# A split weight's low half, made by accumulating transfers instead of GpSimd subtractions

## The chip, the cores and the metric

The kernel runs on one core of one Trainium2 chip. The metric is the device time of one execution in microseconds. It was run three times before the change.

## The reference

One layer of a hybrid encoder, for 256 tokens of width 1024, everything in float32:

```python
u = rmsnorm(h, norm1_w)
rx, rg, qkv, z, a_in, b_in, ga, gb = split_columns(u @ w_in, IN_WIDTHS)
# branch A: convolution, RG-LRU scan, gelu gate, projection
y_a = (gelu(rg) * rglru(conv(rx) + b, ...)) @ w_branch_a
# branch B: convolution + SiLU on q, k, v, chunked gated delta rule, gated norm, projection
y_b = (rmsnorm(gated_delta_rule(q, k, v, g, beta)) * silu(z)) @ w_branch_b
h = h + (sigmoid(ga) * y_a + sigmoid(gb) * y_b) @ w_out
h = h + memory_cross_attention(rmsnorm(h), rmsnorm(mem), w_cq, w_ckv, w_co)
h = h + hierarchical_moe(rmsnorm(h), ...)   # 64 experts, two for each token
return rmsnorm(h, norm_f_w)
```

The products with `w_in`, `w_branch_a`, `w_branch_b`, `w_out`, `w_cq`, `w_ckv` and `w_co` are what the change touches; the experts' weights (3 matrices of 2 MB for each of 64 experts) are not.

## The kernel before

The work has two parts. The first is the dense part: all projections, the two branches, the attention and the router. The second streams the weights of all 64 experts through the chip, in order, and computes each expert on up to 32 gathered tokens.

In the dense part the weights come in 66 units. A unit is one call of `load_w` (L157 to L172): 1024 KB of one weight matrix, 128 partitions by 2048 columns, or 640 KB in the eight units of branch A's projection. SP's queue (L162) loads it into the buffer `raw`, of which there are two. TensorE multiplies numbers of the type fp32r; to keep float32's precision each weight is split into a high half, which is the weight rounded to fp32r, and a low half, which is what the rounding left. The unit is split in two pieces `j`, each in a buffer `whl` of 128 by 2 by 1024: index 0 is the high half, index 1 the low half. There are four such buffers, so a unit uses the two of the unit two before it. ScalarE makes both pieces' high halves (L169). The low half of the first piece is made by VectorE, that of the second by GpSimd (L170), each as `raw` minus the high half.

`dense` (L174 to L180) then does, for each of the k rows of a unit, three matmuls: high weight by high activation (L178), high weight by low activation (L179), low weight by high activation (L180). A unit is two output columns `m` of 8 rows each, so 48 matmuls, or 30 in branch A's projection (one column of 10 rows). Rows 0 to 3 read the first piece, rows 4 to 7 the second: TensorE first reads the second piece's low half in the fifteenth matmul of a unit. L412 to L414 (values of the attention) and L189 to L191 (`dense_two`) are the same three products in other orders.

Which instruction comes when on each engine is decided by a planner that reads the program in order. Where the program says `tc.high_priority()`, as around the split, instructions are put ahead of others that are ready. Semaphores between the engines are added by it. Each engine and each queue works through its list in order; SP's queue holds the raw loads (L162) and the experts' loads (L1068 to L1080). A raw load waits until everything that reads its buffer's old contents is done.

The results of a unit leave PSUM by ScalarE and VectorE. For the convolutions of branch B that is a scaled copy by ScalarE (L309), three multiply-adds by VectorE for each of two columns (L313), a tanh by ScalarE (L462) and two multiply-adds by VectorE (L465). PSUM has four buffers for units.

The dense part's memory is given up in two steps: the early pool before the attention (`estack.close()`), which makes room for four buffers `ra` of 2 MB of expert weights, and the rest (`wstack.close()`) after the last unit, which makes room for six more, `rb`. From then on ten buffers are a ring: after each expert three more loads are issued, into the buffers of loads that are done with.

Of the kernel before, what the change touches and what calls it, by code (L numbers as in the profile page):

```python
# [8 lines left out]
FT = mybir.dt.float32  # L9
FR = mybir.dt.float32r  # L10
I32 = mybir.dt.int32
AF = mybir.ActivationFunctionType
OP = mybir.AluOpType
# [28 lines left out]
def hybrid_kernel(ctx: ExitStack, tc: tile.TileContext, A, out, dbg=None, until=99):  # L42
    nc = tc.nc
    V, SC, G, T = nc.vector, nc.scalar, nc.gpsimd, nc.tensor
# [112 lines left out]
    def load_w(src, k=8, m=256, hi=(SC, SC), lo=(V, G), loads=1):  # L157

        raw = wp.tile([128, 2048], FT, name="raw", bufs=2)[:, :k * m]
        n = k * m // loads  # L160
        for j in range(loads):
            nc.sync.dma_start(raw[:, j * n:(j + 1) * n], src[:, j * n:(j + 1) * n])  # L162
        kh = k // 2
        pieces = []
        with tc.high_priority():
            for j in range(2):
                w = wp.tile([128, 2, 1024], FR, name="whl", bufs=4)[:, :, :kh * m]
                r = raw[:, j * kh * m:(j + 1) * kh * m]
                (hi[j].copy if hi[j] is SC else hi[j].tensor_copy)(w[:, 0], r)  # L169
                lo[j].tensor_sub(w[:, 1], r, w[:, 0].bitcast(FT))  # L170
                pieces.append(w.rearrange("p s (k m) -> p s k m", k=kh))
        return lambda s_, i, ms: pieces[i // kh][:, s_, i % kh, ms]  # L172

# [52 lines left out]
    mt_ = early("memx").rearrange("p (c t) -> p c t", c=8)  # L226
    nc.sync.dma_start(mt_[:, :4], A["memT"][:, :4])
    wkv = [load_w(A["wkv"][0], loads=2)]
    nc.sync.dma_start(mt_[:, 4:], A["memT"][:, 4:])
    um_ = early("umh", FR), early("uml", FR)  # L230
# [25 lines left out]
    for un_ in range(4):  # L256
        w = wkv[0] if un_ == 0 else load_w(A["wkv"][un_])
        p = bank()
        for m in range(2):
            dense(p[:, m * 256:m * 256 + 256], w, m, um)  # L260
        SC.copy(KT[:, 2 * un_:2 * un_ + 2], two(p))
# [57 lines left out]
    def five(name, dt=FT):  # L319
        return early(name, dt)[:, :HB * 256].rearrange("p (b t) -> p b t", b=HB)  # L320
# [25 lines left out]
    for un_ in range(5):  # L346
        w = load_w(A["win"][un_])
        p = bank()
        for m in range(2):
            dense(p[:, m * 256:m * 256 + 256], w, m, u1)  # L350
        for m in range(2):
            r = un_ * 2 + m
            conv(xc[r // HB][:, r % HB], p[:, m * 256:m * 256 + 256], P("rcw", 4 * r, 4), P("rcb", r))
    gg = [five("gg0"), five("gg1")]
    for un_ in range(5):
        w = load_w(A["win"][5 + un_])
# [8 lines left out]
        for m in range(2):  # L365
            r = un_ * 2 + m
# [3 lines left out]
    for h in range(2):  # L370
        tr, ti = five("tr"), five("ti")
        for b in range(HB):
            r = h * HB + b
# [7 lines left out]
        for b in range(HB):  # L381
            r = h * HB + b
# [14 lines left out]
        hi, lo = five("ghh", FR), five("ghl", FR)  # L397
# [6 lines left out]
    for un_ in range(4):  # L404
        w = load_w(A["wkv"][4 + un_])
# [45 lines left out]
    for un_ in range(12):  # L451
        if un_ in (1,):
            z_unit((1,).index(un_))
        w = load_w(A["win"][10 + un_])
# [15 lines left out]
    for m in range(8):  # L470
        w = load_w(A["wa"][m], k=RB, m=128)
# [80 lines left out]
    src = blkT.rearrange("p (s q r) -> p s q r", s=16, q=2)  # L552
# [102 lines left out]
    for c in range(4):  # L655
# [35 lines left out]
        if c < 3:  # L691
# [5 lines left out]
            for h in range(8):  # L697
                src = pS[h % 2][:, h // 2 * 128:h // 2 * 128 + 128]
# [43 lines left out]
    for c0, n in ((0, 2), (2, 2), (4, 2), (6, 1), (7, 1)):  # L742
        if c0 % 2 == 0:
            w = load_w(A["wb"][c0 // 2])
# [22 lines left out]
    for c0, n in ((0, 2), (2, 2), (4, 2), (6, 1), (7, 1)):  # L767
        if c0 % 2 == 0:
            w = load_w(A["wo"][c0 // 2])
# [65 lines left out]
    for un_ in range(4):  # L835
        w = load_w(A["wcq"][un_])
# [43 lines left out]
    for un_ in range(4):  # L880
        w = load_w(A["wco"][un_])
# [522 lines left out]
```

## Time and profile before

| | |
|---|---|
| Median of 3 runs | 1501.56 us (1496.18 to 1501.62) |
| Profiled execution | 1500.7 us, span 1498.9 us |
| TensorE (matmuls) busy | 1113.3 us, 74% of the span |
| VectorE busy | 548.0 us, 37% |
| ScalarE busy | 352.1 us, 23% |
| GpSimd busy | 197.5 us, 13% |
| DMA | 477.40 MB, mean 318 GB/s |
| Chain that ended last | DMA 55% of the span |
| Granted TensorE clock, mean | 0.886 of full speed |

The profile is of one execution. PE is TensorE, DVE is VectorE, ACT is ScalarE, POOL is GpSimd, SP is SyncE, whose queue issues loads. A row of a group names a line of the kernel, the engine, the operation, the tile written and the tiles read, shapes, and how often; a row of a timeline begins with the start and the duration in us. Idle time of an engine is put down to what it waited for.

### The profile page before, as it was taken

How to read it: one execution, taken by the hardware profiler on the slowest of the kernel's cores; microseconds unless marked ns; L12 is line 12 of the kernel's file. 1: busy time of each engine (PE TensorE's matmuls, PEld its weight loads, DVE VectorE, ACT ScalarE, POOL GpSimd, SP SyncE). 2: the span in 40 equal slices, each digit the busy share in tenths (PEclk: the TensorE clock that was granted, in tenths of full speed). 3: DMA queues.
4: the chain of work that ended last, by engine and by line, in shares of the span. 5: the costliest groups of instructions: out<-in, count | busy, mean ns of one | idle time of the engine just before them, and what ended most of it. 6: DMA issues, size and time to landing. Idle time of an engine off the chain costs nothing.

```text
span 1498.9 us, 33205 instructions
## 1 busy us (share of the span) xinstructions
PE 1113.3 (74%) x14941; PEld 932.0 (62%) x14941; DVE 548.0 (37%) x1217; ACT 352.1 (23%) x746; POOL 197.5 (13%) x107
## 2 busy tenths in 40 slices
PE   6899988889999987876666665766656757566575
PEld 5899878779798975654544543544544535354453
DVE  7877688685466532221111211111201111112022
ACT  5356745424444520100000000000000000000011
POOL 2333333441135310000000000000000000000000
PEclk9799999988999998997897888888979889798898
DMA  6343444431147857999999999999999999999995
GB/s 253 118 170 132 138 144 134 148 113 57 38 162 300 327 212 304 426 424 426 426 425 426 425 427 425 425 427 426 425 426 425 427 425 425 426 426 427 426 425 195
DMA packets 42001, 477.40 MB, mean 318 GB/s; under 512 B 4480, under 2 KB 7168, under 8 KB 9856
## 3 DMA queue, kind: packets, MB, share of 16 engines
q1 hardware_dynamic: 40560, 472.56, 77.0%
q8 instruction: 119, 1.95, 0.5%
q10 hardware_dynamic: 1296, 2.68, 0.5%
q14 instruction: 26, 0.21, 0.0%
HBM read 474.17 MB, written 1.05 MB: 317 GB/s over the span
## 4 chain that ended last, share of the span: by engine, by line
DMA 55%; PE 5%; issue 1%; SPq 1%; DVE 0%; ACT 0%; DVEq 0%; ACTq 0%
DMA rb<-weu 11%; DMA rb<-wed 11%; DMA rb<-weg 10%; DMA ra<-wed 10%; DMA ra<-weu 8%; DMA ra<-weg 5%; PE gd L1107 2%; PE gd L1127 1%; PE gd L1098 1%; SPq L1080 1%; PE mm L1175 0%; PE mm L1143 0%; ACT fsq L1296 0%; PE sm L1090 0%; PE gd L1280 0%
## 5 line engine op out<-in xcount | busy, mean ns | idle before, releaser
L1107 PE MATMUL gd<-rb,xy 128*32 128x128 f32 x4864 | 184.0, 317 | 112.8 <-DMA rb<-weu 55.0
L1107 PEld LDWEIGHTS gd<-rb,xy 128*32 128x32 f32 x4864 | 162.2, 128 | 140.1 <-DMA rb<-weu 63.6
L170 POOL TENSOR_TENSOR whl<-raw,whl 128x1024 fp32r<-128x1024 f32 (+1 forms) x66 | 159.8, 2422 | 343.2 <-ACT whl L169 338.3
L1116 DVE SCALAR_TENSOR_TENSOR hid<-hid,gd 128x128 f32<-128x128 f32 x64 | 18.4, 288 | 446.9 <-ACT hid L1115 446.9
L1107 PE MATMUL gd<-ra,xy 128*32 128x128 f32 x3168 | 122.1, 320 | 76.7 <-DMA ra<-weu 39.3
L178 PE MATMUL mm<-u1h,whl 128*128 128x256 f32 x544 | 163.2, 300 | 9.8 <-DVE cvt L313 9.8
L1107 PEld LDWEIGHTS gd<-ra,xy 128*32 128x32 f32 x3168 | 106.9, 129 | 94.5 <-DMA ra<-weu 44.9
L180 PE MATMUL mm<-u1h,whl 128*128 128x256 f32 x544 | 161.3, 297 | 2.6 <-DVE whl L170 2.5
L179 PE MATMUL mm<-u1l,whl 128*128 128x256 f32 x544 | 160.7, 295 | 0.0
L169 ACT CAST whl<-raw 128x1024 fp32r<-128x1024 f32 (+1 forms) x132 | 131.1, 1008 | 105.2 <-PE mm L180 87.7
L1115 ACT ACTIVATE hid<-gd 128x128 f32<-128x128 f32 x64 | 17.8, 278 | 525.0 <-PE gd L1107 525.0
L1132 DVE COPY xy<-gd 32x256 f32<-32x256 f32 x126 | 52.6, 418 | 228.5 <-PE gd L1127 201.9
L1127 PE MATMUL gd<-rb,hid 128*32 128x256 f32 x1216 | 89.8, 445 | 61.4 <-DMA rb<-wed 41.2
L1132 ACT COPY xy<-gd 32x256 f32<-32x256 f32 x126 | 45.9, 364 | 306.0 <-DVE xy L1132 306.0
L178 PEld LDWEIGHTS mm<-u1h,whl 128*128 128x128 f32 x544 | 110.0, 202 | 12.3 <-issue 6.3
L180 PEld LDWEIGHTS mm<-u1h,whl 128*128 128x128 f32 x544 | 109.8, 202 | 5.1 <-DVE whl L170 2.9
L179 PEld LDWEIGHTS mm<-u1l,whl 128*128 128x128 f32 x544 | 109.8, 202 | 0.8 <-issue 0.2
L170 DVE TENSOR_TENSOR whl<-raw,whl 128x1024 fp32r<-128x1024 f32 (+1 forms) x66 | 86.0, 1302 | 55.9 <-ACT whl L169 55.6
L976 POOL TENSOR_TENSOR gpw<-goh,ew 128x512 f32<-128x512 f32 x8 | 8.4, 1049 | 735.2 <-PE sm L1138 680.7
L1127 PEld LDWEIGHTS gd<-rb,hid 128*32 128x32 f32 x1216 | 45.8, 123 | 95.1 <-issue 62.3
L1127 PE MATMUL gd<-ra,hid 128*32 128x256 f32 x800 | 61.1, 456 | 36.5 <-DMA ra<-wed 23.7
L1098 PEld LDWEIGHTS gd<-goh,hm 128*128 128x128 f32 x512 | 61.0, 192 | 14.5 <-issue 14.5
(421 smaller groups left out, 1786.0 us busy)
## 6 DMA issues: line engine op xcount, KB each, us to landing
rb<-weu SPq DMA_DIRECT2D x38, 2048.0 KB, 39.2
rb<-wed SPq DMA_DIRECT2D x38, 2048.0 KB, 39.2
rb<-weg SPq DMA_DIRECT2D x38, 2048.0 KB, 39.1
ra<-weg SPq DMA_DIRECT2D x26, 2048.0 KB, 39.2
ra<-weu SPq DMA_DIRECT2D x25, 2048.0 KB, 39.2
ra<-wed SPq DMA_DIRECT2D x25, 2048.0 KB, 39.2
raw<-win SPq DMA_DIRECT2D x34, 1024.0 KB, 4.9
raw<-wkv SPq DMA_DIRECT2D x7, 1024.0 KB, 5.0
```

Of the source, the lines that this page charges most:

```text
L169: (hi[j].copy if hi[j] is SC else hi[j].tensor_copy)(w[:, 0], r)
L170: lo[j].tensor_sub(w[:, 1], r, w[:, 0].bitcast(FT))
L178: T.matmul(p, w(0, i, ms), u(0, i), start=(i == 0), stop=False)
L179: T.matmul(p, w(0, i, ms), u(1, i), start=False, stop=False)
L180: T.matmul(p, w(1, i, ms), u(0, i), start=False, stop=(i == k - 1))
L1080: nc.sync.dma_start(last_columns(t, q), src[:, q].rearrange("(p j) n -> p j n", p=128))
L1098: T.matmul(o, hm[:, tt, c * 128:c * 128 + 128], g[:, tt], start=(tt == 0), stop=(tt == 1))
L1107: m = T.matmul(p[32 * j:32 * j + 32, o:o + 128], x[:, c], w(c)[:, j * 128:j * 128 + 128], start=(c == 0), stop=(c == 7), tile_position=(0, ...
L1115: SC.activation(tg, p[:, :128], AF.Tanh, scale=0.5)
L1116: V.scalar_tensor_tensor(th, tg, 1.0, p[:, :128], op0=OP.add, op1=OP.mult)
L1127: T.matmul(p[32 * q:32 * q + 32, :256], ht[:, 32 * j:32 * j + 32], w(j)[:, o:o + 256], start=(j == 0), stop=(j == 3), tile_position=(0, 32 ...
L1132: (SC.copy if q % 2 else V.tensor_copy)(Y[r:r + 32, q * 256:q * 256 + 256], p[32 * q:32 * q + 32, :256])
```

## The change

For the pieces whose low half GpSimd made, ScalarE now writes the negated high half into the place of the low half, and a transfer on GpSimd's queue adds the same weights to it, straight from the weight matrix in device memory. The pieces whose low half VectorE makes stay as they are.

```diff
                 (hi[j].copy if hi[j] is SC else hi[j].tensor_copy)(w[:, 0], r)
-                lo[j].tensor_sub(w[:, 1], r, w[:, 0].bitcast(FT))
+                if lo[j] is G:
+
+                    SC.activation(w[:, 1], w[:, 0].bitcast(FT), AF.Copy, scale=-1.0)
+                    G.dma_start(w[:, 1], src[:, j * kh * m:(j + 1) * kh * m], accum_op=OP.add)
+                else:
+                    lo[j].tensor_sub(w[:, 1], r, w[:, 0].bitcast(FT))
                 pieces.append(w.rearrange("p s (k m) -> p s k m", k=kh))
```

## Rows read from the trace of the kernel before

**Rows 1.** The page: span, ScalarE's and GpSimd's load in 40 slices, the subtractions
```profile
span 1498.9 us, 33205 instructions
...
PE 1113.3 (74%) x14941; PEld 932.0 (62%) x14941; DVE 548.0 (37%) x1217; ACT 352.1 (23%) x746; POOL 197.5 (13%) x107
...
ACT  5356745424444520100000000000000000000011
POOL 2333333441135310000000000000000000000000
...
L170 POOL TENSOR_TENSOR whl<-raw,whl 128x1024 fp32r<-128x1024 f32 (+1 forms) x66 | 159.8, 2422 | 343.2 <-ACT whl L169 338.3
```

**Rows 2.** Chain that ended last, in time: start us, us, what
```profile
571.79 1.49 PE gd L1107 x21
...
645.42 38.85 DMA ra<-weg
```

**Rows 3.** Stretches, us: busy us (instructions) by engine, granted clock, DMA share, GB/s
```profile
450.00:500.00 50.00, 46.61 (x366) 45.62 (x365) 34.68 (x47) 23.84 (x35) 29.89 (x23) 0.97 0.83 320
...
550.00:575.00 25.00, 11.09 (x115) 8.14 (x117) 10.23 (x60) 1.78 (x8) 1.50 (x2) 0.63 0.63 255
...
650.00:1450.00 800.00, 518.84 (x9233) 386.21 (x9230) 137.05 (x405) 63.37 (x193) 6.29 (x6) 0.85 1.01 426
```

**Rows 4.** Timelines, one unit at full pace: start us, us, engine, line [idle before]
```profile
83.43 1.05 ACT L169 CAST whl<-raw 128x1024 fp32r<-128x1024 f32 x1 [0.40 <-PE mm L180]
...
84.55 2.40 POOL L170 TENSOR_TENSOR whl<-raw,whl 128x1024 fp32r<-128x1024 f32 x1 [3.35 <-ACT whl L169]
90.31 2.41 POOL L170 TENSOR_TENSOR whl<-raw,whl 128x1024 fp32r<-128x1024 f32 x1 [3.35 <-ACT whl L169]
...
90.61 0.28 PE L180 MATMUL mm<-u1h,whl 128*128 128x256 f32 x1
```

**Rows 5.** One line's instructions: ScalarE activation of 128x1024, ns min/median/max
```profile
L514 ACT ACTIVATE dt<-dt x1: 1053/1053/1053, 295.9 to 295.9; 128x1024 f32<-128x1024 f32 x1
```

**Rows 6.** DMA issues (KB, us to landing), 450 to 500 us last; SP's issue, ns
```profile
raw<-win SPq DMA_DIRECT2D x34, 1024.0 KB, 4.9
...
raw<-wa SPq DMA_DIRECT2D x8, 640.0 KB, 3.8
...
raw<-wo SPq DMA_DIRECT2D x2, 1024.0 KB, 5.7
...
L162 SPq DMA_DIRECT2D raw<-win x34: 327/328/328, 28.9 to 383.3; - x34
```

**Rows 7.** Waits of SP's queue to 600 us: us in total, times, longest
```profile
SPq L162 <- POOL whl L170: 164.3, 54, 10.6
```

**Rows 8.** Timelines, two units with little to spare
```profile
181.20 2.41 POOL L170 TENSOR_TENSOR whl<-raw,whl 128x1024 fp32r<-128x1024 f32 x1 [7.19 <-ACT whl L169]
...
183.66 0.39 PE L180 MATMUL mm<-u1h,whl 128*128 128x256 f32 x1
...
487.63 2.50 POOL L170 TENSOR_TENSOR whl<-raw,whl 128x1024 fp32r<-128x1024 f32 x1 [1.08 <-ACT whl L169]
...
491.18 0.28 PE L180 MATMUL mm<-u2h,whl 128*128 128x256 f32 x1
```

**Rows 9.** Timelines, one unit of branch A's projection
```profile
252.93 0.73 ACT L169 CAST whl<-raw 128x640 fp32r<-128x640 f32 x1 [0.65 <-PE mm L180]
...
258.00 0.28 PE L180 MATMUL mm<-ghh,whl 128*128 128x256 f32 x1
```

**Rows 10.** Timelines of VectorE and GpSimd in the convolutions of branch B
```profile
215.85 0.41 DVE L465 SCALAR_TENSOR_TENSOR kf<-cth,cvt 128x256 f32<-128x256 f32 x1
...
216.58 2.54 DVE L465 SCALAR_TENSOR_TENSOR kf<-cth,cvt 128x256 f32<-128x256 f32 x1
...
216.43 2.40 POOL L170 TENSOR_TENSOR whl<-raw,whl 128x1024 fp32r<-128x1024 f32 x1 [4.83 <-DMA raw<-win]
223.66 2.40 POOL L170 TENSOR_TENSOR whl<-raw,whl 128x1024 fp32r<-128x1024 f32 x1 [4.83 <-ACT whl L169]
```

**Rows 11.** Waits of TensorE to 600 us: us in total, times, longest
```profile
PE mm L178 <- DVE cvt L313: 9.8, 6, 3.7
```

## The prediction, made before the run

> **What bounds the kernel now.** I read the page's heads first, then the chain of waits in order of time, the stretches, the waits of TensorE, and last the timelines of single weight units. The heads show a span in two parts: ScalarE and GpSimd are busy almost only in the first 14 or 15 of 40 slices [rows 1]. The chain shows what ends the span: from 645 us on it is one expert weight transfer behind the other, joined without gaps [rows 2], and between 650 and 1450 us the DMA engines are fully busy at 426 GB/s [rows 3]. That part is bytes divided by rate, and the change leaves its bytes alone. What the change touches lies in the first 15 slices, the dense part with its 66 weight units of `load_w`. How long those take sets when the last staging memory is given up and the first expert can run: between 550 and 575 us the DMA engines are only 0.63 busy and TensorE works 11 of 25 us [rows 3], so nothing there takes up a late start. I therefore pass a delay of the dense part on to the end one to one.
>
> In the dense part TensorE is the bound, and each unit's chain runs beside it. One unit at full pace shows it [rows 4]: ScalarE starts the second half's high part at 83.43 (1.05 us), when TensorE has left the slot; GpSimd subtracts from 84.55 for 2.40 us, to 86.95; TensorE first reads that low half at 90.61. So 3.66 us are to spare, and the next subtraction starts at 90.31: 5.76 us a unit.
>
> **What the change does to this chain.** Per unit it takes away one subtraction on GpSimd (66 of them, 2.42 us on average, 159.8 us in all [rows 1]) and adds one ScalarE pass and one accumulating transfer of 512 KB (320 KB in branch A's eight units), 33 MB in all. None of these 2.42 us is on the path at full pace, so their removal alone is worth nothing there. GpSimd's list waits at the same place as before, one ScalarE pass later; behind it stand only GpSimd's other 38 us of work (197.5-159.8 [rows 1]). A wait for the transfer at L180 is worse placed: TensorE works in order, and all later matmuls stand behind it.
>
> The ScalarE pass costs 1.05 us: the one ACTIVATE of that shape in the trace [rows 5]. The transfer can be issued at 83.43+1.05+1.05+0.07 = 85.60, and must have landed at 90.61. It has 5.0 us, which I call the allowance; D is its time from the end of the ScalarE pass to the landing. If D is longer, TensorE waits. The delay goes around a loop of two units, since a slot is used by every second unit, so at full pace a unit costs (D-5.0)/2.
>
> D has no row of its own. The nearest rows are the raw loads on SP's queue: 4.9 us from issue to landing for 1024 KB, 3.8 for 640 KB [rows 6], so by the line through both 3.4 us for 512 KB. An addition needs the old contents as well; if reading them counts like bytes, the transfer weighs 1024 KB: 4.9. I take 4.2. GpSimd as the issuer has no row either: SP's issue takes 0.33 us [rows 6], already in these figures, and a GpSimd pass over such a tile 2.40 [rows 4]; the extra is between 0 and 2.4 us, and I take 1.0, nearer to SP's, since a request is no pass over data. Third, the raw buffer. SP's next raw load waits for the subtraction on GpSimd in 54 cases [rows 7]. With the change the buffer is free when ScalarE has made the high half, about 1 us ahead of the accumulating transfer, so the 1024 KB load and the addition are in flight together in every unit. The load's own bytes take 1024 KB / 426 GB/s = 2.5 us [rows 3]; sharing costs between 0 and 1.2 us (half of it), I take 0.6. D = 4.2+1.0+0.6 = 5.8 us, with ends at 3.4 and 4.9+2.4+1.2 = 8.5.
>
> The Trainium skill, "Collectives: The Full Stack", section "The bandwidth ceiling: the fold count and why AG ≠ RS ≠ AR", says that an add inside the transfer emits two reads for each write, both on the same ring, and so moves at half a copy's rate. No row here shows it. By it the transfer would weigh 1024 KB, my 4.2 would become 4.9, and the sum would be some 14 us more.
>
> **The sum at D = 5.8.**
> - Units at full pace: I count 25 outside branch A, from the one of rows 4 to the one whose subtraction starts at 487.63 [rows 8], whose low half was ready at most 3.7 us before TensorE read it. Each (5.8-5.0)/2 = 0.4: +10.
> - Branch A's eight units: ScalarE 252.93, 0.73 us a pass, need at 258.00 [rows 9]: allowance 258.00-252.93-2*0.73-0.07 = 3.5. The smaller transfer takes 0.6 less, 5.2. Each (5.2-3.5)/2 = 0.85: +7.
> - Two units where nothing was to spare [rows 8]: 181.20+1.05+5.8 = 188.1 against a need at 183.66, and 487.63+1.05+5.8 = 494.5 against 491.18: 4.4+3.3, less the 0.8 that they have above: +7.
> - A gain: while GpSimd subtracts from 216.43, VectorE's L465 takes 2.54 us where the same instruction took 0.41 a moment before; there the subtractions come every 7.23 us instead of 5.76 [rows 10], and TensorE waits 9.8 us in six waits for VectorE's convolution [rows 11]. With no GpSimd subtraction this stall goes. The next bound is the transfer, 5.76+0.4 = 6.16 a unit. Six units: 6*(7.23-6.16) = -6.4.
> - Between 450 and 500 us the first expert transfers run beside the dense part: DMA share 0.83 [rows 3], a raw load takes 5.7 us there instead of 4.9 [rows 6]. For eight units I add 1 us to D, halved as above: +4 (0 if the load is the later one to suffer, 8 if nothing is halved).
> - ScalarE does 66 more passes in order, 67 us beside the 352 us of [rows 1]. It idled for most of this (it waits on TensorE 0.4 us or more ahead of each high half [rows 4]), but conversions of the convolutions stand behind the new pass. I add 3 (0 to 13: 12 convolution units at 1.05).
>
> Together 10+7+7-6.4+4+3 = +24.6. The profiled execution took 1500.7 us (1498.9 of span), 0.9 under the median shown, so 1500.7+24.6 = 1525, forecast slower.
>
> At D = 3.4 only the tight units wait (2.0+0.9) and six units gain 6*(7.23-5.76) = 8.8: 1495. At D = 8.5: 25*1.75 = 44, branch A (7.9-3.5)/2*8 = 18, tight 13.1-3.5 = 10, convolution +2, the last two terms 7: +81, 1582.
>
> **Rivals.**
> 1. The transfer is hidden, and VectorE's relief is all that is seen. It decides at D = 4.6 and below: no unit at full pace waits. For it: 3.4 us for a plain 512 KB load is inside the allowance of 5.0. Against it: it needs both a cheap addition and a cheap issue, with the raw load now in flight. At D = 3.4 it gives 1495, at 4.6 (5.3 for the tight units, 2 for branch A, 7 for the last two terms, less 8.8) 1506: not slower. The Trainium skill, "DMA: Bandwidth & Descriptors", section "Anatomy of one DMA — SWDGE (gpsimd) path", gives 2.0 us plus bytes at 436 GB/s for a transfer issued by GpSimd, an estimate of 3.2 us here; by it 1494. The raw loads of [rows 6] took 0.3 to 0.5 us more than that formula gives. Chance 0.18, of which 0.05 below 1493.
> 2. The addition is slow, row by row instead of streaming, D = 10. Nothing in the trace speaks for it but that none of its rows adds in flight; against it that every transfer here streams. 25*2.5 = 62, branch A (9.4-3.5)/2*8 = 24, tight 16.1-5 = 11, convolution 6*1 = 6, last terms 7: +110, 1611. Chance 0.14.
> 3. ScalarE becomes the wait: its pass stands ahead of the convolution's first step, VectorE starts 1.05 us late in 12 units, and the relief is lost: 1525+10+6 = 1541. For it: in that stretch L465 and the convolution follow ScalarE closely. Against it: ScalarE is far from full. Chance 0.10.
>
> **How the numbers follow.** My forecast, D between 4.6 and 7.3, has 0.58. About 0.5% (7.5 us) is what a measurement of this kernel can tell from no change. Faster, under 1493: 0.05, the best end of rival 1 with some more relief. Within it: 0.13, the rest of rival 1. Slower: 0.58+0.14+0.10 = 0.82. The range leaves out the lowest end and most of rival 2: 1497 to 1582.
>
> **What would show it.** The time from the accumulating transfer's issue to its landing should be near 5 us, and GpSimd's part of it near 1. TensorE should show a new wait for that transfer at L180, in about 40 units and some 25 us in total; the waits for L313 should shrink from 9.8 to under 4 us, and L465 should have no instance near 2.5. The first expert's matmuls should start some 25 us after 571.79, and the transfers from 650 us on keep 426 GB/s. A wait at L180 with D under 5, or a late dense part without that wait, would make the prediction wrong, as would a gap between the expert transfers.

## The result, and the profile after

The changed kernel took 1578.6 us, the median of four runs (1563.7 to 1587.6), against 1500.2 for the kernel before in the same session: a ratio of 1.050 (95% interval 1.046 to 1.053). One of the four, 1587.6 us, counts as slow and is left out of the ratio and of all differences below, for which the kernel after stands at 1575.8, the median of the other three: slower by 76 us. The profiled executions took 1575.8 and 1500.7: +75. The forecast was +24.6. The direction and the place of the new wait were right; the size was not.

Lines have moved: `dense` is L183 to L185, the negation L172, the transfer L173, VectorE's subtraction L175. The page of the kernel after [rows 1]:

```profile
span 1574.1 us, 33287 instructions
...
PE 1146.4 (73%) x14941; PEld 954.5 (61%) x14941; DVE 480.4 (31%) x1217; ACT 414.6 (26%) x812; POOL 92.8 (6%) x107
```

ScalarE has its 66 passes more (62 us). GpSimd is down to 93 us. VectorE, from which nothing was taken and to which nothing was given, fell from 548 to 480 us; that is the first sign of something my sum undervalued.

From the waits of TensorE to 640 us (us in total, times, longest), those for the transfer. They stand in the place of [rows 11], whose wait for the convolution is gone:

```profile
PE mm L185 <- DMA whl<-win: 28.7, 18, 3.5
PE mm L185 <- DMA whl<-wo: 16.4, 2, 8.6
PE mm L185 <- DMA whl<-wkv: 13.5, 3, 8.7
...
PE mm L185 <- DMA whl<-wa: 9.7, 5, 2.4
PE mm L196 <- DMA whl<-wcq: 7.3, 1, 7.3
...
PE mm L185 <- DMA whl<-wb: 5.6, 3, 2.9
...
PE mm L185 <- DMA whl<-wcq: 2.8, 1, 2.8
PE mm L419 <- DMA whl<-wkv: 2.7, 1, 2.7
```

Together 86.7 us in 34 waits. `w_in` and branch A's `wa` are the ordinary units; the rest are those of `wkv`, with which the kernel begins (13.2 of their 16.2 us are at its first and third unit; the 2.7 at L419 come later), and the ones beside expert loads (`wb`, `wo`, `wcq`).

The DMA issues of the kernel after (KB, median us to landing; raw loads as in [rows 6]):

```profile
raw<-win SPq DMA_DIRECT2D x34, 1024.0 KB, 5.2
whl<-win POOLq DMA_DIRECT2D x34, 512.0 KB, 7.2
...
whl<-wa POOLq DMA_DIRECT2D x8, 320.0 KB, 6.1
...
whl<-wo POOLq DMA_DIRECT2D x4, 512.0 KB, 12.2
whl<-wcq POOLq DMA_DIRECT2D x4, 512.0 KB, 9.8
```

And the transfer's line on GpSimd, its issue (ns min/median/max, first and last start):

```profile
L173 POOL DMA_DIRECT2D whl<-win x34: 853/862/1305, 56.4 to 458.7; - x34
```

One unit at full pace, the counterpart of [rows 4], from the timelines of ScalarE, GpSimd and TensorE (start us, us, [idle before]):

```profile
102.23 1.05 ACT L169 CAST whl<-raw 128x1024 fp32r<-128x1024 f32 x1 [0.39 <-PE mm L185]
...
103.64 1.05 ACT L172 ACTIVATE whl<-whl 128x1024 fp32r<-128x1024 f32 x1
...
104.99 0.86 POOL L173 DMA_DIRECT2D whl<-win  x1 [6.49 <-ACT whl L172]
...
112.66 0.39 PE L185 MATMUL mm<-u1h,whl 128*128 128x256 f32 x1 [2.97 <-DMA whl<-win]
```

The pass ends at 104.69 and TensorE goes on at 112.66: 8.0 us, where I had allowed 5.0 and forecast 5.8.

**Where the 75 us are.** The dense part is the same 3878 matmuls in every kernel. Its stretch to the end of the last unit in the kernel before (columns as in [rows 3]: TensorE, its weight loads, VectorE, ScalarE, GpSimd, clock, DMA share, GB/s):

```profile
0.00:551.30 551.30, 495.62 (x3878) 473.51 (x3879) 370.88 (x661) 271.59 (x500) 188.63 (x98) 0.94 0.45 159
```

The same in the kernel after:

```profile
0.00:626.10 626.10, 513.73 (x3878) 489.22 (x3879) 303.27 (x661) 334.01 (x566) 83.98 (x98) 0.91 0.69 193
```

It is 74.8 us longer: TensorE idles 56.7 us more (112.4 against 55.7), and the same matmuls take 18.1 us more, at a granted clock of 0.91 instead of 0.94. All of this reaches the end. In the chain of waits the first expert starts 74.4 us after the 571.79 of [rows 2]:

```profile
646.18 5.30 PE gd L1112 x128
```

And a late stretch keeps the 426 GB/s of [rows 3]:

```profile
700.00:1500.00 800.00, 528.07 (x9379) 393.02 (x9374) 134.42 (x389) 62.92 (x193) 6.29 (x6) 0.83 1.01 426
```

The clock fell in a long wait. Stretches around one of the first units of the kernel after, TensorE alone (busy us, granted clock, DMA share, GB/s):

```profile
10.00:15.00 5.00, 3.92 (x14) 1.00 1.04 430
15.00:20.00 5.00, 0.00 (x0) 0.80 1.03 366
20.00:25.00 5.00, 1.72 (x8) 0.50 0.74 245
25.00:30.00 5.00, 5.00 (x31) 0.68 0.00 0
30.00:35.00 5.00, 3.59 (x29) 1.00 0.43 118
```

The matmul that ends the wait in them, from TensorE's timeline:

```profile
23.28 0.58 PE L185 MATMUL mm<-umh,whl 128*128 128x256 f32 x1 [8.73 <-DMA whl<-wkv]
```

While TensorE stood for 8.73 us the grant went from 1.00 (2.4 GHz) to 0.50 (1.2 GHz); it was still 0.68 on average over the next stretch, in which TensorE worked without a break, and 1.00 in the one after. This wait cost more than its length.

How much more is not a fixed share of the idle time. The kernel with half the raw bytes, below, idles 90.6 us in its dense part, 35 more than the kernel before, at the same mean grant of 0.94:

```profile
0.00:590.00 590.00, 499.41 (x3878) 475.28 (x3879) 302.68 (x661) 333.58 (x566) 83.92 (x98) 0.94 0.61 149
```

The grant also differs from one execution to the next: another run of the kernel after took 1563.7 us, 12 less than the profiled one, at a mean grant of 0.875 over its span instead of 0.864. Some us of what follows on the clock may be that.

### The profile page after: what moved, and what is told of

The parts are those of the page before. It is cut to its first block, busy times and chain, and to the rows that moved or that the text cites. A ratio compares the mean times of both kernels' runs of the same rounds, so it can differ in the third digit from the quotient of the medians.

```text
span 1574.1 us, 33287 instructions
## 1 busy us (share of the span) xinstructions
PE 1146.4 (73%) x14941; PEld 954.5 (61%) x14941; DVE 480.4 (31%) x1217; ACT 414.6 (26%) x812; POOL 92.8 (6%) x107
## 3 DMA queue, kind: packets, MB, share of 16 engines
q0 software_dynamic: 9504, 33.03, 11.7%
HBM read 507.20 MB, written 1.05 MB: 323 GB/s over the span
## 4 chain that ended last, share of the span: by engine, by line
DMA 53%; PE 5%; DVE 0%; issue 0%; ACT 0%; DVEq 0%; SPq 0%; ACTq 0%
DMA rb<-wed 12%; DMA rb<-weu 10%; DMA ra<-weu 8%; DMA ra<-wed 8%; DMA rb<-weg 8%; DMA ra<-weg 8%; PE gd L1112 2%; PE gd L1132 1%; PE mm L1148 1%; PE gd L1103 1%; PE mm L1180 0%; ACT fsq L1301 0%; PE sm L1095 0%; DVE goh L974 0%; PE gd L1285 0%
## 5 line engine op out<-in xcount | busy, mean ns | idle before, releaser
L185 PE MATMUL mm<-u1h,whl 128*128 128x256 f32 x544 | 163.8, 301 | 28.7 <-DMA whl<-win 28.7
L1112 PE MATMUL gd<-ra,xy 128*32 128x128 f32 x3168 | 126.3, 327 | 67.3 <-DMA ra<-weu 32.8
L183 PE MATMUL mm<-u1h,whl 128*128 128x256 f32 x544 | 162.8, 299 | 1.2 <-ACT sqk L495 1.2
L1112 PEld LDWEIGHTS gd<-ra,xy 128*32 128x32 f32 x3168 | 111.0, 133 | 86.2 <-DMA ra<-weu 38.5
L1132 PE MATMUL gd<-rb,hid 128*32 128x256 f32 x1216 | 101.5, 490 | 63.6 <-DMA rb<-wed 43.4
L185 PEld LDWEIGHTS mm<-u1h,whl 128*128 128x128 f32 x544 | 110.6, 203 | 33.1 <-DMA whl<-win 32.4
L175 DVE TENSOR_TENSOR whl<-raw,whl 128x1024 fp32r<-128x1024 f32 (+1 forms) x66 | 77.6, 1176 | 156.1 <-ACT whl L169 155.9
L183 PEld LDWEIGHTS mm<-u1h,whl 128*128 128x128 f32 x544 | 110.9, 204 | 3.3 <-issue 1.6
L1132 PEld LDWEIGHTS gd<-rb,hid 128*32 128x32 f32 x1216 | 49.9, 134 | 103.4 <-issue 72.1
L1132 PEld LDWEIGHTS gd<-ra,hid 128*32 128x32 f32 x800 | 31.6, 128 | 62.5 <-issue 43.2
L172 ACT ACTIVATE whl<-whl 128x1024 fp32r<-128x1024 f32 (+1 forms) x66 | 66.9, 1016 | 0.7
```

The lines of the kernel that those rows point to most:

```text
L172: SC.activation(w[:, 1], w[:, 0].bitcast(FT), AF.Copy, scale=-1.0)
L183: T.matmul(p, w(0, i, ms), u(0, i), start=(i == 0), stop=False)
L185: T.matmul(p, w(1, i, ms), u(0, i), start=False, stop=(i == k - 1))
L1112: m = T.matmul(p[32 * j:32 * j + 32, o:o + 128], x[:, c], w(c)[:, j * 128:j * 128 + 128], start=(c == 0), stop=(c == 7), tile_position=(0, ...
L1132: T.matmul(p[32 * q:32 * q + 32, :256], ht[:, 32 * j:32 * j + 32], w(j)[:, o:o + 256], start=(j == 0), stop=(j == 3), tile_position=(0, 32 ...
```

## The experiments

The theory: the transfer takes longer than its allowance in many units, for the second read of the addition, the raw load beside it and the crowded stretches. Its rival in size, called V below: much more of the time than I reckoned hangs on VectorE, which GpSimd's subtractions held up, so that both the cost and the relief were larger than in my sum.

**The transfer by itself.** Eight kinds of one transfer, six of each in sequence, in a kernel that does nothing else of the layer:

```diff
+            if beside:
+                nc.sync.dma_start(b, src[i])
+            start(t, src[i][:, 1024:])
...
+    sp = lambda t, s: nc.sync.dma_start(t, s)
+    gc = lambda t, s: G.dma_start(t, s)
+    ga = lambda t, s: G.dma_start(t, s, accum_op=OP.add)
```

> Computes nothing of the layer: a bench of 512 KB transfers on an otherwise idle chip, six of each kind one after the other. SP copy, GpSimd copy, GpSimd copy with the cast to fp32r, GpSimd addition in float32, in fp32r, an addition of half the size, and the fp32r copy and addition beside a 1024 KB load on SP's queue. Theory A (the second read is the price): copy on GpSimd about 4.0 us, addition about 5.3, beside the load 7 for the addition and 5 for the copy. Theory B (GpSimd's issue path is the price): copy and addition on GpSimd both 5.5 to 6, SP's copy 3.4. Theory C (sharing with the raw load): alone all GpSimd transfers under 4.5, the addition beside the load 7.

Its DMA issues (KB, median us to landing); `spcopy` is a copy on SP's queue, `gp...` on GpSimd's, `b...` with a 1024 KB raw load beside it:

```profile
bcopyraw<-win SPq DMA_DIRECT2D x6, 1024.0 KB, 4.9
baddraw<-win SPq DMA_DIRECT2D x6, 1024.0 KB, 5.5
spcopy<-win SPq DMA_DIRECT2D x6, 512.0 KB, 3.7
gpcopy<-win POOLq DMA_DIRECT2D x6, 512.0 KB, 3.9
gpcast<-win POOLq DMA_DIRECT2D x6, 512.0 KB, 4.0
gpadd<-win POOLq DMA_DIRECT2D x6, 512.0 KB, 5.5
...
bcopy<-win POOLq DMA_DIRECT2D x6, 512.0 KB, 5.9
badd<-win POOLq DMA_DIRECT2D x6, 512.0 KB, 7.8
```

So, step by step: 3.7 for the copy (I had 3.4), 0.2 for GpSimd as issuer (1.0), 0.1 for the type, 1.5 for the addition (0.8, being 4.2 less 3.4), 2.3 for the load beside it, from 5.5 to 7.8 (0.6). The issuer was priced too high, the last two far too low. Theory A fits best, but the load beside it costs more than any of the three had. It costs a plain copy 1.9 us too (4.0 to 5.9).

The Trainium skill, "Collectives: The Full Stack", section "The bandwidth ceiling: the fold count and why AG ≠ RS ≠ AR", says of the add in a ReduceScatter that it needs two reads, both on the same ring; the 1.5 us between copy and addition agree with a whole second read of 512 KB (1.2 us at the 426 GB/s of [rows 3]) rather than with my half of one. Its "DMA: Bandwidth & Descriptors", section "Anatomy of one DMA — SWDGE (gpsimd) path", gives an estimate of 3.2 us for 512 KB; the copy took 3.9, and the addition, of which that section does not speak, 5.5.

**No transfer.** The low half stays the negated high half; all other work stays.

```diff
-                    G.dma_start(w[:, 1], src[:, j * kh * m:(j + 1) * kh * m], accum_op=OP.add)
```

> The changed kernel without the transfer: the low half of the second piece stays the negated high half, so the weights' second half is left out of it. Theory L (the loss is TensorE's wait for the transfer, ScalarE's pass is free): all waits at the low-half matmuls go, and VectorE is freed of GpSimd's subtractions: 1488 to 1497 us, 0.3 to 0.8% faster than before. Rival S (ScalarE's pass in front of other work costs): 1510 to 1540.

1448.2 us, ratio to before 0.966 (0.962 to 0.969), far below both expected ranges. Its dense stretch:

```profile
0.00:499.00 499.00, 474.81 (x3878) 455.37 (x3879) 298.90 (x661) 332.48 (x566) 26.64 (x32) 0.98 0.49 176
```

This parts the change in two. Adding the transfers lengthens the dense part from 499.0 to 626.1: +127.1, of which 88.2 is idle time of TensorE (24.2 to 112.4; the waits listed above sum to 86.7) and 38.9 slower matmuls (474.8 to 513.7, clock 0.98 to 0.91). Taking GpSimd's subtractions away, with ScalarE's 66 passes already in, is worth 551.3-499.0 = 52.3: 31.5 idle, 20.8 slower matmuls. My sum had +31 and -6.4 for the two. The ScalarE passes can cost little: of the 24.2 us that TensorE idles here, 11.7 are waits for ScalarE's high halves, and 10.1 of these are the one before the first unit, which the kernel before has too.

**The transfer without its second read.** A copy of the weights into the low half's place, without the addition:

```diff
-                    G.dma_start(w[:, 1], src[:, j * kh * m:(j + 1) * kh * m], accum_op=OP.add)
+                    G.dma_start(w[:, 1], src[:, j * kh * m:(j + 1) * kh * m])
```

> The changed kernel with the transfer as a plain copy: the low half of the second piece becomes the whole weight, so the negated high half is left out of it. Theory A: D falls by the price of the second read, from 7.2 to about 5.7, and TensorE's waits for it from 87 us to about 40: 1530 us. Theory B: D stays at 6.5 to 7, 1555 to 1570.

1521.7 us, ratio 1.013 (1.009 to 1.017), 54 under the kernel after and less than Theory A's 1530: the addition is some four tenths of the 127. Its DMA issues:

```profile
whl<-win POOLq DMA_DIRECT2D x34, 512.0 KB, 5.2
```

From its waits of TensorE, the units of `w_in`:

```profile
PE mm L185 <- DMA whl<-win: 10.4, 11, 2.3
```

2.0 us less per transfer is what the probe has with a load beside it, 1.9 (7.8 against 5.9), and more than its 1.5 without one. (Some 0.3 us of it may be GpSimd's issue, which takes 0.53 us here and 0.86 in the kernel after.) The DMA queues (packets, MB, share of 16 engines' span) say the same. GpSimd's in the kernel after:

```profile
q0 software_dynamic: 9504, 33.03, 11.7%
```

In the kernel with the copy, for the same bytes:

```profile
q0 software_dynamic: 9504, 33.03, 6.7%
```

**The negation first.** It reads the raw weights, and it and the transfer are put ahead of that piece's high half:

```diff
-                (hi[j].copy if hi[j] is SC else hi[j].tensor_copy)(w[:, 0], r)
                 if lo[j] is G:
-
-                    SC.activation(w[:, 1], w[:, 0].bitcast(FT), AF.Copy, scale=-1.0)
+                    SC.activation(w[:, 1], r, AF.Copy, scale=-1.0)
                     G.dma_start(w[:, 1], src[:, j * kh * m:(j + 1) * kh * m], accum_op=OP.add)
+                    (hi[j].copy if hi[j] is SC else hi[j].tensor_copy)(w[:, 0], r)
                 else:
+                    (hi[j].copy if hi[j] is SC else hi[j].tensor_copy)(w[:, 0], r)
                     lo[j].tensor_sub(w[:, 1], r, w[:, 0].bitcast(FT))
```

(Here the negated number is the weight rounded by ScalarE in that pass.)

> The changed kernel with the negation read from the raw weights and put ahead of the second piece's high half, the same values; the transfer is issued 1.05 us earlier, and 1.5 us where a convolution's copy stood in between. Theory L, loop of two units: each waiting unit gains half of that, 0.5 to 0.75 us, some 40 units: 20 to 30 us, 1545 to 1555. Rival (the transfers are late because the DMA engines are full, so an earlier issue only waits longer): no change, 1570 to 1578.

1557.8 us (1547.6 to 1567.4), ratio 1.038 (1.031 to 1.045): 18 us under the kernel after, less than the 20 to 30 expected. The single runs of the two kernels overlap and the intervals of their ratios only just do not, so the gain is small and its size uncertain. Starting 1.05 us earlier was partly given back, for the DMA issues show both transfers slower, the raw load at 7.7 and the addition at 8.1:

```profile
raw<-win SPq DMA_DIRECT2D x34, 1024.0 KB, 7.7
whl<-win POOLq DMA_DIRECT2D x34, 512.0 KB, 8.1
```

**Half the raw bytes.** The raw load brings only the first half of the unit, which serves both pieces:

```diff
-            nc.sync.dma_start(raw[:, j * n:(j + 1) * n], src[:, j * n:(j + 1) * n])
+            if j * 2 < loads:
+                nc.sync.dma_start(raw[:, :k * m // 2], src[:, :k * m // 2])
...
-                r = raw[:, j * kh * m:(j + 1) * kh * m]
+                r = raw[:, :kh * m]
```

> The changed kernel with raw loads of half the bytes: the first piece's raw weights serve for both pieces' high halves, so the second piece's high half is of other weights. The accumulating transfer stays. Theory (1.8 to 2.4 us of D = 7.2 are the raw load beside it): D falls to 6.0 to 6.4, each unit at full pace gains 0.4 to 0.6 and the crowded units more: 1545 to 1558. Rival (raw loads do not slow it): D 7.0 to 7.2, 1570 to 1578.

1544.4 us, ratio 1.033 (1.029 to 1.037), 31 under the kernel after; the addition lands after 6.3 instead of 7.2. Sharing the engines with the raw load is real, and half of that load is worth 0.9 us of each transfer:

```profile
whl<-win POOLq DMA_DIRECT2D x34, 512.0 KB, 6.3
```

**Subtraction back in the crowded units.** `wb`, `wo` and `wcq`, 12 of the 66 units, are split on GpSimd as before:

```diff
-    def load_w(src, k=8, m=256, hi=(SC, SC), lo=(V, G), loads=1):
+    def load_w(src, k=8, m=256, hi=(SC, SC), lo=(V, G), loads=1, acc=True):
...
-                if lo[j] is G:
+                if lo[j] is G and acc:
...
-            w = load_w(A["wb"][c0 // 2])
+            w = load_w(A["wb"][c0 // 2], acc=False)
...
```

> The change undone in 12 units, those of w_branch_b, w_out and w_cq, where expert transfers already run beside the dense part; there GpSimd subtracts again. Their waits for the transfer are 32 us in the changed kernel (5.6, 16.4, 7.3 and 2.8). Theory (expert transfers make these units the costliest): 1540 to 1548. Rival (a wait taken away here comes back as a later start of the expert transfers, or GpSimd's subtractions block VectorE): 1555 to 1578.

1541.2 us (1530.9 to 1552.0), ratio 1.030 (1.025 to 1.035), 35 under the kernel after. The waits for these units summed to 32.1 us. A fifth of the units thus carries over a quarter of the transfers' 127 us.

**GpSimd busy, its results unused.** To the kernel without transfers, GpSimd gets its subtractions back, as two of 128x512 each, into a scratch tile that nothing reads:

```diff
+    scratch = cp.tile([128, 512], FT, name="scratch")
...
+                    for q in range(2):
+                        hs = slice(q * kh * m // 2, (q + 1) * kh * m // 2)
+                        G.tensor_sub(scratch[:, :kh * m // 2], r[:, hs], w[:, 0, hs].bitcast(FT))
```

> The kernel without the transfer (1448 us), to which GpSimd's subtractions are given back as work that nobody waits for: in each unit two subtractions of 128x512 read the raw weights and the high half and write into a scratch tile; the second piece's low half stays the negated high half. Theory V (the 50 us between the kernel before and the one without the transfer are VectorE blocked while GpSimd subtracts): 1485 to 1502 us, L465 again near 2.5 us. Rival P (they are TensorE's wait for GpSimd's low half, or the planner's other order): 1448 to 1460.

1490.4 us, ratio to before 0.995 (0.993 to 0.997): 42 of the 52 us are back, though no result of GpSimd is used. One thing does wait for these subtractions, as in [rows 7]: the next raw load, since they read its buffer. From the waits of SP's queue:

```profile
SPq L164 <- POOL scratch L177: 159.0, 62, 4.8
```

Little of the 42 can come by that way: ScalarE's waits for raw weights grow from 1.0 us without the subtractions to 11.4, so by that row it is some 10 us at most. VectorE's busy time goes from 476 to 536 us with the same 1217 instructions. Its L465, here L474 (ns min/median/max), is slow again [rows 10]:

```profile
L474 DVE SCALAR_TENSOR_TENSOR kf<-cth,cvt x8: 412/756/1491, 204.8 to 223.6; 128x256 f32<-128x256 f32 x8
```

The same line in the kernel after, L470, is not:

```profile
L470 DVE SCALAR_TENSOR_TENSOR kf<-cth,cvt x8: 415/418/427, 231.7 to 250.1; 128x256 f32<-128x256 f32 x8
```

The slowest is now 1.49 instead of 2.54 us, as each subtraction is half as long. That is the form a blocking has: an instruction waits for the rest of the other's. (L465 had been expected near 2.5 again.)

**Both low halves on VectorE.** The kernel before, GpSimd's subtractions given to the engine that they held up:

```diff
-    def load_w(src, k=8, m=256, hi=(SC, SC), lo=(V, G), loads=1):
+    def load_w(src, k=8, m=256, hi=(SC, SC), lo=(V, V), loads=1):
```

> The kernel before with both low halves on VectorE, none on GpSimd and no transfer; the reference's result. Theory V: VectorE takes 1.2 us a unit more for the subtraction and loses the blocked time, up to 2.1 us a unit where it worked beside GpSimd's: 1455 to 1485, faster than both. Rival P: VectorE's added 77 us land on its own chain, 1500 to 1530.

1460.4 us, the median of six runs (1453.5 to 1464.2), ratio to before 0.974 (0.972 to 0.976). It is faster than both kernels. From its page:

```profile
PE 1110.5 (76%) x14941; PEld 925.2 (63%) x14941; DVE 541.3 (37%) x1283; ACT 353.3 (24%) x746; POOL 38.6 (3%) x41
```

Its subtractions among VectorE's groups (busy us, mean ns | idle before):

```profile
L170 DVE TENSOR_TENSOR whl<-raw,whl 128x1024 fp32r<-128x1024 f32 (+1 forms) x132 | 153.8, 1174 | 58.8 <-ACT whl L169 58.2
```

The same group in the kernel before, and two others of it:

```profile
L170 DVE TENSOR_TENSOR whl<-raw,whl 128x1024 fp32r<-128x1024 f32 (+1 forms) x66 | 86.0, 1302 | 55.9 <-ACT whl L169 55.6
...
L363 DVE SCALAR_TENSOR_TENSOR gsq<-gsq,gxx 128x512 f32<-128x512 f32 x5 | 10.1, 2024 | 4.7 <-ACT gxx L362 4.7
L753 DVE TENSOR_TENSOR mrg<-mrg,ya 128x512 f32<-128x512 f32 (+1 forms) x5 | 9.9, 1979 | 0.1
```

VectorE does 66 subtractions more, 67.8 us of work, and is busy 6.7 us less (541.3 against 548.0). Each of its own takes 1.17 instead of 1.30 us, and lines far from the convolution, L363 and L753, took some 2 us in the kernel before. Here the longest of either is 0.68, as the line of the first shows (ns min/median/max):

```profile
L363 DVE SCALAR_TENSOR_TENSOR gsq<-gsq,gxx x5: 683/683/684, 94.4 to 116.9; 128x512 f32<-128x512 f32 x5
```

## Why the prediction was right or wrong

**Right: direction, place and path.** TensorE waits for the low half in the second half of a unit (L185), ScalarE's added pass is hidden (or nearly), the wait at L313 and the slow L465 are gone, and the delay of the dense part passes to the end one to one: 74.8 us at the last unit, 74.4 at the first expert, 75.1 at the end. GpSimd's issue, 0.86 us, is near the 1 us that I named for it. The direction owes something to chance all the same: it is what was left of two terms of opposite sign that were both far too small.

**Right: the loop over two units.** With the measured landing, 7.2 us after an issue some 0.3 us behind the pass, my own (D-5.0)/2 gives 1.25 us a unit, 31 for 25 units; the waits of `w_in` sum to 28.7. (The sum fits, the spread does not: 18 waits, of up to 3.5 us, not 25 alike.) For branch A, (6.1+0.3-3.5)/2*8 = 12, measured 9.7.

**Wrong: "D = 4.2+1.0+0.6 = 5.8".** Near 7.5 here. I took an addition as half a second read; it is a whole one (1.5 us in the probe, 2.0 in the kernel). I took 0.6 of at most 1.2 for the raw load; it was 2.3 in the probe, beyond my own bound, which came from two transfers sharing the load's 2.5 us evenly. That bound fails for a plain copy already (1.9); why is not shown. The extra for GpSimd as issuer, where I had put most of the doubt, is 0.2. Full pace and branch A came to 38 us instead of 17.

**Wrong: "eight units, +4" and the tight units, +7.** The crowded ones (`wb`, `wo`, `wcq`) cost 32 us of waits. A transfer of `wo` lands after 12.2 us and one of `wcq` after 9.8, not D+1, and the two waits for `wo` are of 8 us each, not halved. What became of the two tight units one by one is not worked out; of these, the second had 1.05 us to spare, not nothing (487.63+2.50 = 490.13, read at 491.18 [rows 8]), which leaves the +7 as it is. The units of `wkv` (16 us) stood in no term: at the first of them TensorE had done 14 matmuls when it stood for 8.73 us.

**Missing: the clock.** I priced each wait at its length. The granted clock was lower too, as around the first wait above, and the same matmuls took 39 us longer than without transfers. This alone is more than my whole forecast.

**Wrong: "six units, -6.4".** I saw the blocked L465 in one stretch and priced that stretch. GpSimd's subtractions held VectorE up in the whole dense part. Without them the kernel was 52 us faster, and 42 of these came back when GpSimd subtracted for nobody. The page had the sign of it: a VectorE line of 128x512 elements at 2.02 us where one of 128x1024 takes 1.30.

The Trainium skill, "SBUF — State Buffer", section "Who interferes with whom", says that a VectorE instruction with two inputs in that memory contends with a GpSimd instruction that reads it, that such contention is an exclusive lock, and that the order of issue decides who blocks. L465 (2.54 against 0.41 us [rows 10]) and its 1.49 beside subtractions of half the length agree. It gives no price; the 42 us of the scratch experiment are one for this kernel.

So the sum should have read 38 (ordinary units) + 32 (crowded) + 16 (`wkv`) + 2 (the rest of the idle time) + 39 (clock) - 52 (relief) = +75. Both large terms were some four to eight times mine, with opposite signs, and the error that was left, 50 us, is smaller than either.

What stays open: 10 of the 52 us of relief did not come back with the scratch subtractions. These are of another shape, and smaller. Waits for GpSimd's low halves themselves are not the reason: in the kernel before, TensorE's idle time ahead of L180 that ended with such a low half (us, times) is

```profile
POOL whl L170: 0.3, 1
```

How much of the 39 us of clock belongs to which waits is open as well. A fifth `whl` buffer, which would lengthen the allowance, was not tried.

## What to carry to other kernels

Before moving work off GpSimd, sum up what VectorE loses beside it: compare one instruction's minimum and maximum by line, over the whole stretch and not at one place; here giving VectorE the work itself was faster than every other kernel tried that makes the same low halves. A transfer that adds took 1.5 us longer than a copy alone and 2.3 longer again beside a load, so it belongs where a unit has slack for some 8 us, not where the slack is 5. And where TensorE is the bound, price a new wait at more than its length: the granted clock can fall in it.

## What was not expected of the hardware

- A 512 KB addition in flight beside a 1024 KB load lands after 7.8 us, alone after 5.5, a copy after 3.9; the load beside it goes from 4.9 (beside a copy) to 5.5.
- GpSimd as the issuer of a plain copy costs only 0.2 us over SP (3.9 against 3.7), although its issue takes 0.53 us of its own time for a copy, and 0.86 for an addition.
- VectorE is busy less with 132 subtractions of its own than with 66 beside GpSimd's 66 (541.3 against 548.0 us).
